# A list scheduler's price table: same-bank PSUM reads put in sequence, a charge for the return to dense products, and other durations re-set

## The chip, the core and the metric

The kernel runs on one core of a Trainium2 chip. Its time is device microseconds (us) from start to end of one execution; three runs of the kernel before are known. One execution was also profiled, and every instruction of it has a start and a duration in the trace. The engines are called as in the profile: PE (TensorE, with PEld for its weight loads), DVE (VectorE), ACT (ScalarE), POOL (GpSimd) and SP (SyncE, which issues the DMAs).

## The reference

One layer of a streaming encoder, for a prompt of 1024 rows and a sample of 32 rows (1056 columns in all, model width 1024), everything in float32:

```
n = rmsnorm(x);  p = n @ w_in                        # 1024 x 3840
x += concat(hgrn2(p[:, :2048]), rwkv7(p[:, 2048:])) @ w_out
x += cross_attention(rmsnorm(x), memory K/V)         # 4 heads of 256, 256 memory rows
x += (silu(n @ w_ff1) * (n @ w_ff3)) @ w_ff2         # n = rmsnorm(x), hidden width 2816
y = rmsnorm(x)
```

`hgrn2` and `rwkv7` are recurrences over time. The kernel computes both by chunks: many small products, element-wise work between them, and a state that goes from chunk to chunk. Memory K and V of the prompt are two more products (`w_ck`, `w_cv`). States, shift rows and memory K/V are outputs too.

## The kernel before

**Products.** A float32 product of full width is made of three float32r products: each operand is split into a high part (an ACT copy) and a low part (a DVE or POOL subtraction), and hi*hi, hi*lo and lo*hi are added up in one PSUM bank (`gemm`, L778; `load_w`, L764; `split`, L798). These are called **dense** here. They have 352 moving columns in the projections, `w_out` and `w_cq`, 264 in `w_co` and the feed-forward part (there with a seven-product scheme, `fast`, L1140), 256 in the memory K/V products. All others are **short** products of the recurrences, the transposes and the attention, in float32 or float16, many on a 64-row or 64-column part of the array.

**Stages.** `run` (L852) records the stages one after the other: the mixers (`mixers`, L1363: the 30 projections of `w_in`, and for each of four head pairs `rwkv`, L1489, and `hgrn`, L1737, each over five pieces of time); memory K/V (`memory_kv`, L886); `out_proj` (L946); `cross` (L962); `ff_hidden` (L1167) and `ff_out` (L1267); `final` (L1338). In the mixers the recurrences are chains of short products with DVE, ACT and POOL work between them, and the dense projections of the next head pairs run beside them on PE. Two places in the chains matter here:

- `inverse` (L1667) inverts small triangular matrices, level by level. At each of four levels DVE reads a PSUM bank to place it on a block diagonal (`place(xbd, ps, self.both)`, L1723; 128x512 in float16) and ACT reads the same bank to copy it (`S.copy(x, ps)`, L1725; 128x256 to float16).
- the state chain of `rwkv` (L1610 to L1628) has three links in each chunk of 64 rows: products `ps_b`, DVE addition; products `ps_sa`, one copy by DVE from partitions 0 to 63 and one by ACT from 64 to 127; products `ps_h`, a DVE multiply-add. The next chunk begins with the result.

**What sets the order.** Nothing is issued while stages are recorded. Each call makes a node of a graph (`record`, L322); `touch` (L161) adds an edge between two nodes that use overlapping parts of one buffer, if one of them writes. A few products in a row are one PE node. Then a list scheduler (`order`, L376) plays the engines forward with clocks of its own: each node costs what `price` (L218) says, an engine switch adds `wait` (L206, table `DELAY`), and a node with a second price, "late", lets its engine go on at once while its result counts as ready later. At each step the engine whose clock is earliest takes, of the nodes that are ready at that clock, the one with the longest remaining path (L557), if buffers and PSUM banks are to be had (`fits`, L490). A stage may start early only when few enough nodes of the earlier stages are left (`LEAD`, L493: 1100 for memory K/V, 250 for `out_proj`). Memory K/V and the projections have a large bias that puts them behind everything else that is ready, so that they fill what is free on PE. The charge for a change of products on PE (`change`, L278) is added to a PE node's cost after the node has been picked (L573).

The result is a fixed order of instructions for each engine, SP included. Every engine runs its own in this order and waits where its next instruction waits, so the planner's prices bear on the chip only through the order. All instructions are emitted by one helper line (L365), so the profile names them by tiles: `bank` is a PSUM bank; `r`, `rw`, `f`, `mb`, `ma`, `wr` are regions of SBUF (`r` holds activations, `rw` split weights, `wr` raw weights, `f`, `mb` and `ma` the rest). A dense projection product is `bank<-r,rw 128x352`; a memory K/V product is `bank<-rw,ma 128x256`.

## Time and profile before

| what | value |
|---|---|
| median of 3 runs | 1962.35 us (1960.7 to 1963.19) |
| time of the profiled execution | 1963.09 us |
| span of its trace (first to last instruction) | 1961.0 us |
| PE busy | 1868.9 us, 95% of the span |
| DVE, ACT, POOL busy | 1402.3, 837.6, 654.7 us |
| mean granted TensorE clock | 0.986 of full speed |

How to read the rows that follow: a row of the windows gives, for a stretch of the span, its length and each engine's busy time in it with the count of instructions, then the granted clock (1.00 is full), the share of time that the DMA engines were busy, and GB/s. A row of the timeline gives the start, the length, the engine, the line, the operation with its tiles and shape, how many equal ones follow each other (x6), and in square brackets how long the engine was idle before and what ended that. A row of the groups ends with the busy time in us, the mean of one instruction in ns, and the idle time before them.

### The profile page before, as it was taken

The numbers are of one execution on the slowest core, as the hardware profiler recorded it, in microseconds if no ns is written. First come the engines' busy times: TensorE is split into PE (matmuls) and PEld (weight loads), VectorE is DVE, ScalarE is ACT, GpSimd is POOL, SyncE is SP. The second block draws the span as 40 slices with busy tenths as digits, with TensorE's granted clock in tenths as the row PEclk, the third lists the DMA queues.
The fourth block names the chain that finished last, engine by engine and source line by source line (L and its number), as shares of the span: only waits on it lengthen the run. The fifth ranks groups of instructions, "written<-read, shape, count | busy, mean of one in ns | idle before, by whom it ended". The sixth has DMA issues, their size and how long they took to land. (4 is left out here: it accounts for less than half of the span.)

```text
span 1961.0 us, 40641 instructions
## 1 busy us (share of the span) xinstructions
PE 1868.9 (95%) x15785; PEld 1731.9 (88%) x15785; DVE 1402.3 (72%) x3112; ACT 837.6 (43%) x2151; POOL 654.7 (33%) x926
## 2 busy tenths in 40 slices
PE   6899999999999999899999999899999999999998
PEld 6788888887788878789899999799999999999997
DVE  4786789659857875634555456797777877968997
ACT  4553545454545455633222235533233333464432
POOL 4632444135424532105400014632332433322421
PEclk9899999999999999899999999899999999999999
DMA  4100110011001101641112122222233224465622
GB/s 144 34 12 26 41 41 23 4 53 29 23 28 45 35 7 52 199 152 34 43 56 64 33 63 88 70 81 93 91 111 117 83 83 137 144 181 168 183 89 89
DMA packets 158111, 149.51 MB, mean 76 GB/s; under 512 B 10080, under 2 KB 146400, under 8 KB 157920
## 3 DMA queue, kind: packets, MB, share of 16 engines
q1 hardware_dynamic: 157920, 146.93, 23.8%
q8 instruction: 124, 2.03, 0.4%
q14 instruction: 67, 0.55, 0.1%
HBM read 111.02 MB, written 35.88 MB: 75 GB/s over the span
## 5 line engine op out<-in xcount | busy, mean ns | idle before, releaser
L365 PE MATMUL bank<-r,rw 128*128 128x264 f32 (+1 forms) x5808 | 928.7, 310 | 29.0 <-DVE rw L365 10.6
L365 PEld LDWEIGHTS bank<-r,rw 128*128 128x128 f32 x5808 | 824.9, 190 | 49.4 <-DVE rw L365 12.3
L365 PE MATMUL bank<-mb,rw 128*128 128x264 f32 (+3 forms) x3456 | 484.4, 293 | 9.0 <-DVE rw L365 7.6
L365 PEld LDWEIGHTS bank<-mb,rw 128*128 128x128 f32 x3456 | 455.9, 189 | 17.4 <-DVE rw L365 11.7
L365 DVE TENSOR_TENSOR f<-bank,f 128x264 f32<-128x264 f32 (+11 forms) x798 | 317.4, 421 | 121.1 <-PE bank L365 114.9
L365 PE MATMUL bank<-f 64*64 64x64 f32 (+8 forms) x2472 | 278.2, 256 | 30.3 <-DVE f L365 14.3
L365 PEld LDWEIGHTS bank<-f 64*64 64x64 f32 (+5 forms) x1675 | 167.2, 155 | 65.4 <-DVE f L365 18.4
L365 POOL TENSOR_TENSOR f<-f 128x2 f32<-128x2 f32 (+8 forms) x167 | 104.6, 637 | 318.9 <-ACT f L365 242.0
L365 ACT ACTIVATE f<-f 128x256 f32<-128x256 f32 (+7 forms) x392 | 158.3, 423 | 112.3 <-DVE f L365 87.5
L365 ACT CAST rw<-wr 128x512 fp32r<-128x512 f32 (+3 forms) x167 | 116.1, 700 | 209.5 <-PE bank L365 132.1
L365 DVE TENSOR_TENSOR f<-f 128x264 f32<-128x264 f32 (+10 forms) x266 | 187.0, 716 | 25.1 <-POOL f L365 12.0
L365 DVE TENSOR_TENSOR rw<-wr,rw 128x512 fp32r<-128x512 f32 (+3 forms) x137 | 109.6, 805 | 43.8 <-ACT rw L365 43.0
L365 ACT CAST rw<-ma 128x512 fp32r<-128x512 f32 (+2 forms) x124 | 70.9, 573 | 153.8 <-POOL ma L365 85.8
L365 ACT COPY f<-bank 128x264 f32<-128x264 f32 (+6 forms) x251 | 87.4, 361 | 111.7 <-PE bank L365 99.6
L365 DVE TENSOR_TENSOR rw<-ma,rw 128x512 fp32r<-128x512 f32 (+2 forms) x124 | 82.5, 672 | 34.2 <-ACT rw L365 34.1
L365 POOL TENSOR_SCALAR f<-f 128x64 f32<-128x64 f32 (+6 forms) x117 | 49.1, 421 | 172.8 <-DVE f L365 104.8
L365 PE MATMUL bank<-f,mb 64*64 64x64 f32 (+9 forms) x982 | 84.9, 241 | 3.8 <-DVE f L365 2.4
L365 ACT CAST f<-bank 128x256 f16<-128x256 f32 (+1 forms) x144 | 46.5, 339 | 87.8 <-PE bank L365 56.9
L365 POOL TENSOR_TENSOR ma<-ma 128x512 f32<-128x512 f32 (+4 forms) x41 | 52.5, 1283 | 90.3 <-DVE rw L365 89.9
L365 ACT ACTIVATE f<-bank,f 128x256 f32<-128x256 f32 (+4 forms) x127 | 52.6, 430 | 69.6 <-DVE f L365 31.2
L365 POOL TENSOR_TENSOR ma<-wr 128x512 f32<-128x512 f32 (+1 forms) x13 | 25.0, 1927 | 161.9 <-DVE rw L365 95.2
L365 DVE TENSOR_TENSOR f<-bank,r 128x264 f32<-128x264 f32 (+1 forms) x56 | 25.2, 464 | 71.8 <-PE bank L365 64.7
(189 smaller groups left out, 2269.2 us busy)
## 6 DMA issues: line engine op xcount, KB each, us to landing
wr<-in_w_in_dram SPq DMA_DIRECT2D x30, 512.0 KB
wr<-in_w_ff_dram SPq DMA_DIRECT2D x27, 512.0 KB
ma<-in_w_ff_dram SPq DMA_DIRECT2D x25, 512.0 KB
h_scratch<-f SPq DMA_DIRECT2D x18, 528.0 KB
f<-h_scratch SPq DMA_DIRECT2D x36, 264.0 KB
ma<-h_scratch SPq DMA_DIRECT2D x34, 264.0 KB
h_scratch<-f SPq DMA_DIRECT2D x12, 396.0 KB
f<-mix_scratch SPq DMA_DIRECT2D x24, 176.0 KB
```

Of the source, the lines that this page charges most:

```text
L365: getattr(eng, method)(*args, **kw)
```

## The change

Only the planner's numbers and edges change; what is computed, the nodes, the buffers and the rule of picking stay.

- `touch` also adds an edge between two reads of overlapping parts of one PSUM bank by different engines, in the order of recording.
- `change` no longer adds 0.03 us wherever either neighbour on PE is not dense; it adds 0.1 us where a dense node follows a short product of certain kinds (`short`).
- An ACT instruction's price goes from 0.18 us (PSUM) or 0.21 us (SBUF) plus 0.83 ns a column to 0.06 or 0.11 us plus the same, with 0.1 us "late".
- POOL's prices change by operation and type, and `DELAY` for ACT and POOL; a DMA is priced at 300 GB/s in place of 200, landing 2.1 us later in place of 1.9.

```diff
-SWITCH, SMALL = 0.095, 0.03
+SWITCH, HIDE = 0.095, 0.1
...
-            if (write or w) and n is not node:
+            if (write or w or self.space == "PS" and n.eng != node.eng) and n is not node:
...
-DELAY = {("vector", "tensor"): 0.2, ("vector", "gpsimd"): 0.18, "vector": 0.115, ("scalar", "tensor"): 0.1,
-         ("scalar", "gpsimd"): 0.05, "scalar": 0.02, ("gpsimd", "tensor"): 0.08, "gpsimd": 0.0, "tensor": 0.21,
+DELAY = {("vector", "tensor"): 0.2, ("vector", "gpsimd"): 0.18, "vector": 0.115, ("scalar", "tensor"): 0.07,
+         ("scalar", "gpsimd"): 0.09, "scalar": 0.04, ("gpsimd", "tensor"): 0.08, "gpsimd": 0.04, "tensor": 0.21,
...
-        return max(0.4, n * out.shape[0] * 4 / 200e3), 1.9
+        return max(0.42, n * out.shape[0] * 4 / 300e3), 2.1
...
-        return (0.18 if args[1].buf.space == "PS" else 0.21) + n * 0.83e-3 + (0.095 if pointer else 0.0), 0.0
+        return (0.06 if args[1].buf.space == "PS" else 0.11) + n * 0.83e-3 + (0.095 if pointer else 0.0), 0.1
     if method == "affine_select":
-        return 0.35, 0.0
+        return 0.36, 0.0
     if method == "memset":
-        return 0.06 + n * 0.5e-3, 0.0
+        return 0.1 + n * 0.8e-3, 0.0
     if method == "tensor_tensor":
-        return 0.13 + n * 2.12e-3 + (0.45 if args[3] == ALU.pow else 0.0), 0.0
+        rounded = out.dtype == F32R and n < 512 or out.dtype == F32 and n in (384, 512)
+        return 0.18 + n * (2.85e-3 if rounded else 2.2e-3) + (0.45 if args[3] == ALU.pow else 0.0), 0.0
     if method == "tensor_scalar":
-        return 0.3 + n * (2.9e-3 if args[4] == ALU.max else 1.3e-3), 0.0
-    return 0.24 + n * 1e-3, 0.0
+        return 0.24 + n * (3.3e-3 if args[4] == ALU.max else 1.1e-3), 0.0
+    return 0.18 + n * 1e-3, 0.0
...
+def short(call):
+    method, args, kw = call
+    if method == "transpose":
+        return args[1].shape[0] <= 64
+    lhs, rhs = kw["lhsT"], kw["rhs"]
+    return lhs.dtype != F32R and (lhs.dtype == F16 or cut_of_array(call) != (False, False) or math.prod(rhs.shape[1:]) < 128)
+
 def change(a, b):
     if a is None:
         return 0.0
-    return (SWITCH if cut_of_array(a.calls[-1]) != cut_of_array(b.calls[0]) else 0.0) + (0.0 if a.dense and b.dense else SMALL)
+    return (SWITCH if cut_of_array(a.calls[-1]) != cut_of_array(b.calls[0]) else 0.0) + (HIDE if b.dense and short(a.calls[-1]) else 0.0)
```

## The prediction

> **What bounds the kernel now.** I read the page first (span and busy time), then the windows, then the waits of PE.
>
> ```profile
> span 1961.0 us, 40641 instructions
> PE 1868.9 (95%) x15785; PEld 1731.9 (88%) x15785; DVE 1402.3 (72%) x3112; ACT 837.6 (43%) x2151; POOL 654.7 (33%) x926
> ```
>
> PE is busy for all but 92.1 us of the span (1961.0 less 1868.9). The change removes no product, so what it can win is idle PE time, and what it can lose is more of it. The windows tell where the 92.1 us lie:
>
> ```profile
> 0.00:100.00 100.00, 77.90 (x481) 71.38 (x482) 58.92 (x129) 51.40 (x122) 54.90 (x127) 0.95 0.30 92
> 100.00:200.00 100.00, 94.77 (x1110) 82.67 (x1110) 75.43 (x184) 47.72 (x139) 31.55 (x69) 0.97 0.05 14
> 200.00:700.00 500.00, 486.51 (x4975) 412.42 (x4974) 381.43 (x1047) 251.65 (x776) 212.49 (x384) 1.00 0.11 32
> 786.00:846.00 60.00, 46.90 (x346) 43.07 (x347) 35.90 (x77) 36.41 (x89) 7.36 (x16) 0.90 0.63 197
> 900.00:1200.00 300.00, 293.77 (x1872) 279.07 (x1871) 157.73 (x377) 93.87 (x226) 55.16 (x54) 0.99 0.17 53
> 1200.00:1300.00 100.00, 87.75 (x649) 84.60 (x648) 81.16 (x143) 50.90 (x125) 50.90 (x44) 0.93 0.21 68
> 1300.00:1700.00 400.00, 396.61 (x3228) 393.45 (x3227) 314.75 (x487) 131.84 (x241) 135.84 (x76) 1.00 0.31 105
> 1700.00:1961.00 261.00, 245.76 (x1930) 239.61 (x1928) 221.74 (x453) 112.06 (x259) 73.33 (x91) 0.99 0.47 145
> ```
>
> The start has 22.1 us of it, the rest of the mixers up to 700 us 18.7 (5.2 and 13.5), their end and memory K/V 13.1, the way into the feed-forward part 12.2, and the last 261 us 15.2. The middle of the mixers, where the planner mixes most, is already 97% busy. That is the frame: no plan can win more than some tens of us.
>
> **The change part by part.** The planner's prices act through the order alone, so I compared the two built orders, engine by engine.
>
> *The charge for a return.* Dense products follow each other every 0.161 us (41 of them from 914.79 to 921.39, 6.60 us):
>
> ```profile
> 914.79 1.45 PE L365 MATMUL bank<-mb,rw 128*128 128x352 f32 x8
> ...
> 921.39 0.65 PE L365 MATMUL bank<-mb,rw 128*128 128x352 f32 x3
> ...
> 251.81 1.23 PE L365 MATMUL bank<-r,rw 128*128 128x352 f32 x6
> 252.88 0.27 PE L365 MATMUL bank<-f 128*32 128x128 f32 x1
> ```
>
> Six of them after short products took 1.07 us to the next start, 0.97 by that spacing: a return costs 0.10, as the new charge says. But the charge is added after a node is picked, so it can't make returns fewer, and it doesn't: the new order has 354 returns, the old 352, and 718 changes between array cuts against 717. Two more at 0.10 are +0.2 us. I take it as nothing.
>
> *Two reads of one bank.* They are in sequence on the chip already. DVE placed from 734.29 to 734.98, ACT began 0.04 us after:
>
> ```profile
> 734.29 0.69 DVE L365 TENSOR_TENSOR mb<-bank,f 128x512 f16<-128x512 f32 x1 [0.33 <-PE bank L365]
> 735.02 0.37 ACT L365 CAST f<-bank 128x256 f16<-128x256 f32 x1 [0.66 <-DVE mb L365]
> ```
>
> The new edges are 116: 36 in the attention, between a maximum and the exponential that needs it anyway, and the 80 of `inverse`. In the old order ACT came first in 25 of the 80; now DVE always does. The ACT copy can come 0.69 us later by that, but its reader waits for two more products and the next placement (another 0.69) in any case: nothing. The two copies of the state chain read different partitions of one bank, so they get no edge, and the planner still has them side by side.
>
> *The durations.* An ACT instruction on 256 columns lasts 0.40 to 0.42 us, but the next one starts after 0.32 and 0.31:
>
> ```profile
> 144.08 0.42 ACT L365 ACTIVATE f<-f 128x256 f32<-128x256 f32 x1 [0.28 <-DVE f L365]
> 144.40 0.40 ACT L365 ACTIVATE ma<-ma 128x256 f32<-128x256 f32 x1
> 144.71 0.40 ACT L365 ACTIVATE f<-f 128x256 f32<-128x256 f32 x1
> ...
> L365 POOL TENSOR_TENSOR r<-f,r 128x352 fp32r<-128x352 f32 x24 | 29.0, 1225 | 92.2 <-DVE f L365 61.4 <-ACT r L365 30.8
> ```
>
> The old price holds ACT for 0.42 us, the new one for 0.32 and 0.1 late: the trace is with the new. A rounded POOL subtraction of 352 columns takes 1.225 us; 0.88 was planned, 1.18 now is. So the plan comes nearer to the chip, and its order differs nearly everywhere in the mixers. From 857 us on it differs little. What this is worth I work out at the places where PE waits.
>
> *Start to the first chains.*
>
> ```profile
> 85.67 0.33 PE L365 MATMUL bank<-f,mb 64*64 64x64 f32 x4 [0.66 <-POOL f L365]
> 89.61 0.70 PE L365 MATMUL bank<-f 128*128 128x256 f32 x2 [3.61 <-DVE f L365]
> 91.13 1.22 PE L365 MATMUL bank<-f 128*128 128x256 f32 x2 [0.82 <-DVE f L365]
> ...
> 141.47 0.40 PE L365 MATMUL bank<-f 64*64 64x64 f32 x4 [1.78 <-DVE f L365]
> 142.41 3.99 PE L365 MATMUL bank<-mb 128*64 128x64 f32 x34 [0.55 <-DVE mb L365]
> ```
>
> The release of the product at 91.13 stands behind 111 DVE instructions in the new order, 115 in the old, with as much PE work before it. Four at about 0.4 us are 1.6; I take **-1.5** (0 to -4.4, the waits of 3.61 and 0.82). In the first state chain the old order has three links with no dense product between them (from 139 to 142.4); the new has a group of six between every two of the first links, 0.97 us each. That covers the 0.55 and half of the 1.78: **-1.5** (0 to -2.3), though what fills here is missing later.
>
> *The middle, 150 to 700 us.* Idle time is 13.5 us in 200 to 700, in many waits under 2 us. The 135 or so links of the state chains that have under 1 us of PE work ahead of them fall from 21 to 17. In that share, 19% of 13.5, it is -2.6; I take **-2** (-8 if truer durations cover most, +4 if the new mix only moves the waits).
>
> *The end of the mixers* is where the new order looks worse.
>
> ```profile
> 781.69 1.12 PE L365 MATMUL bank<-r,rw 128*128 128x352 f32 x6
> 782.64 3.00 PE L365 MATMUL bank<-rw,ma 128*128 128x256 f32 x24
> ...
> 756.72 8.57 SPq L365 DMA_DIRECT2D f<-in_w_ck_dram  x2
> ...
> 797.26 0.47 PE L365 MATMUL bank<-f 128*128 128x128 f32 x1 [3.37 <-ACT f L365]
> ...
> 780.00:790.00 10.00, 8.85 (x67) 8.23 (x66) 9.07 (x25) 7.72 (x21) 3.69 (x8) 1.00 0.62 190
> 790.00:800.00 10.00, 4.83 (x35) 3.85 (x34) 6.46 (x16) 7.24 (x23) 2.46 (x7) 0.85 0.65 194
> 800.00:810.00 10.00, 7.46 (x37) 6.91 (x38) 8.63 (x23) 6.50 (x17) 1.58 (x4) 0.64 0.59 180
> ```
>
> In the old order the last projection is followed at once by memory K/V, whose first two weight tiles had been issued from 756.72 us on, and 51 short products are left to go between. In the new one the projections end earlier, 115 short products follow with nothing dense among them, and the first memory weights are issued only after two tiles of `w_out` and five of `out_proj`'s operands. By the median spacing of such products in the trace these 115 are 18.7 us of PE work. The nearest stretch of before, 780 to 810, is 70% busy (21.14 of 30): 18.7 at 70% is 26.7, a loss of 8.0. Against it, 38 short products fewer than before are left beside memory K/V, and the old 8.9 us of idle there shrinks; I take half, -4.4. Two weight tiles of 512 KB more then go through a stretch that moves 197 GB/s: 1.05 MB, 5.3 us if the transfers bind there; the DMA engines are 63% busy, so I take +1.4. Sum **+5** (-3 if the old idle goes wholly and the DMA doesn't bind, +14 with the 8.0, the 5.3 and some clock).
>
> [...]
>
> ```profile
> 793.00:800.00 7.00, 1.83 (x10) 1.05 (x9) 4.15 (x10) 6.39 (x20) 2.46 (x7) 0.78 0.69 211
> 800.00:804.00 4.00, 2.66 (x10) 2.37 (x11) 3.96 (x11) 3.60 (x12) 0.29 (x1) 0.50 0.57 188
> ```
>
> After seven us in which PE worked for 1.83, the granted clock was 0.50 for the next four. [...]
>
> *Into the feed-forward part.*
>
> ```profile
> 1228.40 5.21 PE L365 MATMUL bank<-r,rw 128*128 128x264 f32 x22 [3.35 <-DVE rw L365]
> ...
> 1251.00:1295.00 44.00, 38.05 (x291) 37.21 (x292) 36.76 (x53) 17.47 (x35) 19.87 (x18) 0.96 0.12 37
> ```
>
> The DVE instruction that releases 1228.40 is number 2081 on DVE in the old order, 2071 in the new: ten fewer ahead, enough to end the 3.35. But the releases near 1251, 1260 and 1295 have the same numbers in both (2118 and 2119, 2127, 2167), and DVE is busy for 36.76 of those 44 us. What isn't done before is owed there: I take **-1** (-3.4 to 0). From there the orders agree but for small moves: 0.
>
> Sum: -1.5 - 1.5 - 2 + 5 - 1 = -1.0 us. On the profiled execution (1963.09, its span and 2.1 around it) that is 1962.1; it ran 0.74 above the median of the three, so on the median 1962.35 it is 1961.3. I predict **1961.0**.
>
> **The rivals.**
> - *The truer plan wins through the mixers.* All its small terms come out at their good ends: -4.4, -2.3, -8, and the end of the mixers costs nothing: -14.7, 1948. For it: ACT and POOL rows, and the thicker chain. Against it: 97% busy there already.
> - *PE runs out of fill* (slower). One place: the 115 short products at the mixers' end. The 8.0 and 5.3 with no return, and 2.7 for ten us at clocks near 0.6: +16; less the 5 us won elsewhere, +11, 1973. It decides if PE is under about 75% busy in that run. For it: 790 to 800 above. Against it: several chains end there together and can cover each other.
> - *The change does nothing that can be measured*: the charge is no part of the pick, 36 of 116 edges are void, and waits only move. That is my forecast's neighbourhood: within 0.2%, about what a measurement of this kernel can tell from no change (1958.4 to 1966.3).
>
> **How the numbers follow.** My forecast, waits that move and cancel (1955 to 1967), gets 0.42: 0.09 of it under 1958.4, 0.31 within, 0.02 above. The truer plan (1943 to 1955) gets 0.27, the lack of fill (1967 to 1980) 0.31. So faster 0.36, same 0.31, slower 0.33. Both signs hold much of the chance; the range takes in most of both, 1945 to 1976.
>
> **What would show it.** Right: PE idle of 15 to 20 us in the 100 us from the last `bank<-r,rw 128x352` of the mixers to `out_proj`, up from 13.1 in 786 to 846; waits gone near 140 and at the first 264-column products; the same idle later. Wrong: a mixers' end as full as before (then the first rival), or memory K/V products that wait for DMA (then the second). If idle time changes after 1300 us, I have missed where the orders differ.

## The result, and the profile after

The changed kernel takes 1968.97 us (median of 8 runs, 1966.92 to 1974.39) against 1962.19 us for the kernel before, measured beside it (8 runs): ratio 1.0036, 95% interval 1.0024 to 1.0049. It is slower, by 6.8 us or 0.36%: a small loss, but 1 lies outside the interval. I had put 0.42 on waits that move and cancel, 1961.0 us; the time lies in the range of 1945 to 1976.

The page of the changed kernel, span and busy time:

```profile
span 1967.9 us, 40633 instructions
...
PE 1874.4 (95%) x15785; PEld 1735.9 (88%) x15785; DVE 1406.3 (71%) x3112; ACT 826.1 (42%) x2150; POOL 666.0 (34%) x926
```

PE was idle for 92.1 us before (1961.0 less 1868.9) and is now for 93.5 (1967.9 less 1874.4). So of 6.9 us of span only 1.4 are idle time, and 5.5 are a PE that is *busy* for longer with the same 15785 products. That already says where to look: at the granted clock. Its mean over the profiled execution is 0.986 before and 0.977 after; as the clock records of both traces hold only 1.00 and 0.50, that is about 55 and 91 us at half clock. The windows, in the columns of the prediction (length, busy PE, PEld, DVE, ACT, POOL, granted clock, DMA share, GB/s):

```profile
0.00:100.00 100.00, 82.25 (x550) 74.94 (x550) 63.52 (x140) 51.08 (x125) 59.08 (x133) 0.95 0.30 92
100.00:200.00 100.00, 96.14 (x1138) 82.43 (x1137) 81.45 (x211) 52.41 (x167) 36.76 (x76) 1.00 0.07 19
200.00:700.00 500.00, 480.12 (x4838) 407.10 (x4838) 367.29 (x1005) 239.59 (x751) 204.19 (x367) 0.98 0.10 31
786.00:846.00 60.00, 49.26 (x329) 45.03 (x330) 37.26 (x92) 36.79 (x101) 11.09 (x25) 0.77 0.70 218
900.00:1200.00 300.00, 292.31 (x1844) 277.89 (x1843) 157.63 (x372) 93.72 (x227) 59.19 (x56) 0.99 0.17 53
1200.00:1300.00 100.00, 88.38 (x659) 85.18 (x658) 79.37 (x139) 54.21 (x132) 50.96 (x46) 0.93 0.21 65
1300.00:1700.00 400.00, 396.83 (x3228) 394.72 (x3227) 315.36 (x490) 129.13 (x234) 140.84 (x76) 1.00 0.31 105
1700.00:1967.00 267.00, 251.99 (x1988) 245.37 (x1986) 228.55 (x464) 115.65 (x267) 78.41 (x93) 0.99 0.46 144
```

Against the rows of before: up to 200 us PE is idle for 21.6 us in place of 27.3; from 200 to 700 for 19.9 in place of 13.5; from 786 to 846 for only 10.7 in place of 13.1, but at a clock of 0.77 in place of 0.90. From 900 us on nothing differs by over 1.5 us.

Windows at fixed times compare different work. So here and below I also use the **extra time** at a point of PE's work: the products are counted in their order, each at the median distance between starts that its kind has in the trace of before (a dense 352-column one 0.161 us), and the extra time is the start of the product there less that sum. Waits, slow clocks and slow releases are all in it.

| stretch of PE's work, us | extra before | extra after | difference | the prediction's terms there |
|---|---|---|---|---|
| 0 to 150 | 45.2 | 33.7 | -11.5 | -1.5 and -1.5 |
| 150 to 650 | 31.3 | 44.1 | +12.8 | -2 |
| 650 to 750 | 19.8 | 27.6 | +7.8 | +5 |
| 750 to the end | 51.9 | 51.0 | -0.9 | -1 |

With 1.7 us less work by that count (1803.1 against 1801.4) this is +6.5, of the 6.9 by which the spans differ. The change wins more at the start than I thought possible, gives all of it back in the middle, and loses at the mixers' end. How the loss divides between the second and the third row depends on how finely the kinds of product are told apart; by coarser kinds more of it falls to the second.

**The start.** Both kernels, 0 to 160 us (before first):

```profile
0.00:160.00 160.00, 132.87 (x1127) 119.67 (x1128) 109.57 (x245) 81.41 (x204) 79.12 (x172) 0.95 0.21 65
```

```profile
0.00:160.00 160.00, 139.47 (x1300) 124.66 (x1301) 117.01 (x263) 85.61 (x222) 84.72 (x177) 0.97 0.21 65
```

In the same 160 us PE starts 1300 products in place of 1127, and DVE is busy for 7.4 us more.

**The middle.** Before, from 160 to 350 and from 600 to 660 us, and the same of the changed kernel:

```profile
160.00:350.00 190.00, 187.23 (x2008) 158.61 (x2008) 148.38 (x403) 98.65 (x306) 79.46 (x151) 1.00 0.10 28
...
600.00:660.00 60.00, 58.31 (x554) 49.88 (x553) 46.12 (x127) 25.83 (x83) 33.78 (x55) 1.00 0.18 53
```

```profile
160.00:350.00 190.00, 180.65 (x1865) 152.78 (x1864) 141.96 (x395) 92.60 (x296) 74.83 (x147) 0.98 0.10 28
...
600.00:660.00 60.00, 55.03 (x431) 48.41 (x431) 48.15 (x120) 25.28 (x80) 33.59 (x58) 0.91 0.16 47
```

Both stretches lose busy time and clock. The worst place in the first, in the timeline of PE and the windows of the changed kernel:

```profile
316.61 0.29 PE L375 MATMUL bank<-f,ma 128*128 128x64 f16 x4
...
320.14 0.33 PE L375 MATMUL bank<-f 64*64 64x64 f32 x4 [1.44 <-DVE f L375]
...
322.25 0.58 PE L375 MATMUL bank<-ma 128*128 128x64 f16 x8 [1.56 <-DVE ma L375]
...
328.89 1.23 PE L375 MATMUL bank<-r,rw 128*128 128x352 f32 x6
...
320.00:325.00 5.00, 3.30 (x37) 2.85 (x38) 4.97 (x13) 3.05 (x7) 2.63 (x7) 0.57 0.00 0
325.00:330.00 5.00, 4.66 (x54) 3.42 (x52) 4.47 (x13) 1.74 (x4) 4.81 (x4) 0.75 0.31 90
```

From 316.6 to 328.9 PE starts no dense product, DVE is busy for 9.44 of the 10 us from 320 to 330, and the clock is at half from 320.7 to 327.5. The worst place in the second:

```profile
641.38 3.13 DVE L375 SCALAR_TENSOR_TENSOR f<-f 128x256 f32<-128x256 f32 x1
...
641.82 2.33 POOL L375 TENSOR_TENSOR rw<-wr,rw 128x1024 fp32r<-128x1024 f32 x1
...
645.17 3.81 PE L375 MATMUL bank<-f 128*128 128x64 f16 x39 [2.62 <-DVE f L375]
648.91 2.13 PE L375 MATMUL bank<-r,rw 128*128 128x352 f32 x6
```

A DVE instruction on 256 columns lasts 3.13 us (the 66 of its kind and shape in the kernel before take 0.54 us in the mean), and ends 0.36 us after a POOL subtraction on 1024 columns that began beside it. PE has no dense product from 640.7 to 648.9, waits 2.62 us for DVE, and is at half clock from 644.9 to 651.8.

**The end of the mixers.** The timeline of PE (last projection, short products, first memory K/V product) and of SP:

```profile
773.47 1.21 PE L375 MATMUL bank<-r,rw 128*128 128x352 f32 x6
...
794.14 2.16 PE L375 MATMUL bank<-f 128*128 128x128 f32 x7 [5.86 <-DVE f L375]
797.52 0.79 PE L375 MATMUL bank<-f 128*128 128x128 f32 x2 [1.23 <-DVE f L375]
...
800.84 9.19 PE L375 MATMUL bank<-f 128*128 128x128 f32 x42
809.68 0.56 PE L375 MATMUL bank<-rw,ma 128*128 128x256 f32 x1
```

```profile
790.23 5.81 SPq L375 DMA_DIRECT2D f<-mix_scratch  x5
...
802.54 0.38 SPq L375 DMA_DIRECT2D f<-in_w_ck_dram  x1
```

```profile
788.00:800.00 12.00, 4.88 (x20) 3.42 (x20) 7.98 (x29) 6.31 (x23) 4.29 (x13) 0.51 0.61 180
800.00:805.00 5.00, 5.00 (x26) 4.52 (x27) 2.94 (x9) 3.52 (x13) 0.41 (x2) 0.50 0.24 77
805.00:810.00 5.00, 5.00 (x25) 4.59 (x24) 2.60 (x8) 2.72 (x9) 0.94 (x2) 0.50 0.63 188
810.00:816.00 6.00, 4.57 (x23) 4.33 (x22) 4.64 (x13) 3.73 (x17) 3.10 (x4) 0.53 0.72 226
816.00:826.00 10.00, 9.98 (x78) 8.89 (x77) 6.15 (x12) 7.18 (x16) 0.95 (x2) 1.00 0.83 258
```

The last projection ends at 774.7 us, and the first load of memory K/V's weights is issued only at 802.54, 27.8 us later (before: at 756.72, 26 us *ahead* of the last projection's end at 782.8). In between PE has short products alone, stands still for 5.86 us up to 794.14, and is at half clock from 788.3 on, for 27.3 us. From 800 to 810 it is busy all the time, and still at 0.50.

### The profile page after: what moved, and what is told of

It is laid out like the page before. It is cut to its first block, busy times and chain, and to the rows that moved or that the text cites. A ratio compares the mean times of both kernels' runs of the same rounds, so it can differ in the third digit from the quotient of the medians.

```text
span 1967.9 us, 40633 instructions
## 1 busy us (share of the span) xinstructions
PE 1874.4 (95%) x15785; PEld 1735.9 (88%) x15785; DVE 1406.3 (71%) x3112; ACT 826.1 (42%) x2150; POOL 666.0 (34%) x926
## 4 chain that ended last, share of the span: by engine, by line
PE 72%; DVE 16%; issue 4%; POOL 4%; ACT 3%; DMA 1%; DVEq 0%; ACTq 0%; SPq 0%; POOLq 0%
PE bank L375 72%; DVE f L375 9%; POOL f L375 2%; DVE rw L375 2%; DVE ma L375 2%; DVE mb L375 2%; ACT f L375 2%; POOL mb L375 1%; DMA f<-h_scratch 1%; ACT mb L375 1%; POOL rw L375 0%; DVE r L375 0%; ACT rw L375 0%; POOL ma L375 0%; ACT ma L375 0%
## 5 line engine op out<-in xcount | busy, mean ns | idle before, releaser
L375 PE MATMUL bank<-r,rw 128*128 128x264 f32 (+1 forms) x5856 | 945.6, 311 | 27.9 <-DVE rw L375 9.4
L375 PE MATMUL bank<-mb,rw 128*128 128x264 f32 (+4 forms) x3408 | 478.6, 293 | 7.2 <-DVE rw L375 6.5
L375 DVE TENSOR_TENSOR f<-bank,f 128x264 f32<-128x264 f32 (+10 forms) x766 | 310.2, 426 | 153.2 <-PE bank L375 146.0
L375 PE MATMUL bank<-f 128*128 128x64 f16 (+7 forms) x2574 | 287.1, 258 | 34.9 <-DVE f L375 21.7
L375 PEld LDWEIGHTS bank<-f 128*128 128x128 f32 (+3 forms) x1718 | 173.6, 160 | 69.6 <-DVE f L375 23.4
L375 POOL TENSOR_TENSOR f<-f 128x2 f32<-128x2 f32 (+7 forms) x160 | 101.8, 647 | 298.1 <-ACT f L375 241.6
L375 DVE TENSOR_TENSOR f<-f 128x264 f32<-128x264 f32 (+9 forms) x224 | 136.7, 623 | 14.5 <-POOL f L375 6.0
L375 PEld LDWEIGHTS bank<-f,mb 128*128 128x128 f32 (+6 forms) x874 | 62.5, 147 | 22.0 <-DVE f L375 7.3
L375 ACT CAST rw<-f 128x512 fp32r<-128x512 f32 (+3 forms) x71 | 45.9, 650 | 80.1 <-PE bank L375 70.1
L375 DVE TENSOR_TENSOR ma<-bank,f 128x512 f16<-128x512 f32 (+9 forms) x139 | 61.8, 458 | 24.6 <-PE bank L375 23.8
L375 ACT ACTIVATE f<-bank,f 128x256 f32<-128x256 f32 (+4 forms) x127 | 52.4, 431 | 59.3 <-DVE f L375 33.4
```

The costliest lines, as they stand in the source:

```text
L375: getattr(eng, method)(*args, **kw)
```

## The experiments

The theories, which the expectations spell out further: *gap*, that the loss is the stretch at the mixers' end in which PE has only short products; *prices*, that one part of the change costs by itself; *draw*, that each set of prices draws another order, whose losses have little to do with the prices' truth. Two more came up on the way: *page*, that what counts at the mixers' end is when the first weights of memory K/V are loaded, and *rows*, that the loads and splits of memory K/V's rows disturb the middle. The table gathers all runs; extra time is as above, from one profiled run each, and the last column is the issue of the first memory K/V load against the end of the last projection, in us.

| kernel | median, us | ratio to before, 95% | extra 0-150 | 150-650 | 650-750 | first load |
|---|---|---|---|---|---|---|
| before | 1962.2 | | 45.2 | 31.3 | 19.8 | -26.1 |
| after | 1969.0 | 1.0024 to 1.0049 | 33.7 | 44.1 | 27.6 | +27.8 |
| e1 charge alone | 1994.6 | 1.0145 to 1.0176 | 45.7 | 40.6 | 47.0 | +41.5 |
| e2 before, 1 ns | 1993.4 | 1.0147 to 1.0182 | 52.4 | 41.3 | 38.4 | +33.0 |
| e3 without charge | 1951.4 | 0.9924 to 0.9951 | 35.1 | 37.6 | 16.1 | -18.5 |
| e4 fill | 1976.5 | 1.0054 to 1.0081 | 36.9 | 44.3 | 22.8 | +16.5 |
| e9 charge 0.11 | 1956.3 | 0.9959 to 0.9983 | 34.4 | 29.0 | 27.2 | -5.1 |
| e10 charge 0.095 | 1971.9 | 1.0034 to 1.0080 | 37.0 | 30.3 | 37.9 | +62.7 |
| e6 GpSimd alone | 1970.8 | 1.0027 to 1.0058 | 43.2 | 34.1 | 22.8 | -13.0 |
| e5 read order alone | 1985.3 | 1.0094 to 1.0130 | 44.9 | 48.1 | 33.6 | +1.9 |
| e11 after, free page | 1960.2 | 0.9976 to 0.9999 | 36.9 | 47.5 | 17.3 | -65.8 |
| e12 before, free page | 1963.5 | 0.9997 to 1.0016 | 43.0 | 32.1 | 20.5 | -79.2 |
| e13 before, late load | 1976.8 | 1.0053 to 1.0083 | 44.5 | 30.5 | 35.7 | +15.9 |
| e14 read order, free page | 1976.6 | 1.0051 to 1.0085 | 46.8 | 44.7 | 29.7 | -74.9 |
| e15 charge 0.11, free page | 1951.8 | 0.9928 to 0.9953 | 31.9 | 37.7 | 18.7 | -70.2 |
| e16 ScalarE and DMA | 2008.3 | 1.0206 to 1.0263 | 46.0 | 51.3 | 40.4 | +42.2 |
| e7 DMA alone | 1989.6 | 1.0121 to 1.0148 | 42.1 | 40.6 | 34.9 | +27.7 |
| e17 after, rows late | 1958.2 | 0.9966 to 0.9987 | 36.4 | 44.9 | 11.9 | -75.2 |
| e18 without GpSimd | 1958.3 | 0.9970 to 0.9991 | 32.8 | 28.2 | 18.7 | -8.1 |
| e19 without read order | 1978.1 | 1.0068 to 1.0099 | 42.0 | 50.0 | 25.9 | +2.4 |

How far can one profiled run be trusted? Three runs with the order of before up to 686 us of work (before, e12, e13) have 31.3, 32.1 and 30.5 in the second column; four with that of the changed kernel up to 571 (after, e4, e11, e17) 44.1, 44.3, 47.5 and 44.9. But e9 and e15 share an order up to 678 and have 29.0 and 37.7. A difference under 9 us in that column is not told from chance here; the 12.8 between before and after is, as three runs of the one order and four of the other lie apart.

### The charge by itself, one nanosecond, and the change without the charge

e1 is the kernel before with the new `change` and `short`, nothing else. e3 is the changed kernel with the old `change` (SMALL = 0.03). e2 is the kernel before with the price of a float16 product raised by 1 ns:

```diff
-            return max(0.029, n / 2400 + 0.002), 0.0
+            return max(0.029, n / 2400 + 0.003), 0.0
```

> Only the charge for a return to dense products is changed, the other prices and edges are as before. Its built order has the same feature as the changed kernel: after the last projection 19.1 us of short products stand on PE with no dense product among them (18.7 in the changed kernel, none before). Theory 'gap' (this run of short products, through idle PE and the half clock that follows it, is what makes the change slower): half-speed clock for 15 us or more in that stretch, and 1964 to 1972 us. Theory 'prices' (a price nearer to the trace makes a better plan; the slower end comes from another part of the change): at or under 1962 us. Theory 'every plan is a new draw' (any shift of the planner's clocks gives another order, several us up or down through the whole mixers): a time anywhere from 1954 to 1974, not tied to the gap.

> The kernel before with one planned duration raised by 1 ns (a float16 product, 0.003 in place of 0.002 us of fixed cost): no price is nearer to the trace by that in any way that counts. Its order has a gap of 17.6 us of short products after the last projection. 'Gap': 1964 to 1971 us with a half-speed spell of 15 us or more at the end of the mixers. 'Prices': as before, 1960 to 1964 us. 'Every plan is a new draw': anywhere from 1954 to 1974.

> The whole change without the new charge (the old charge stays). Its order has a gap of 0.8 us, and the first memory K/V weights are issued early, as before. 'Gap': the early gain of the changed kernel (12.7 us at its best, near 157 us) may or may not last, but the end of the mixers costs no more than before (17.9 us of PE time over its work from the last projection to the first product of out_proj), and the kernel is at or under 1963 us. 'Prices': between the changed kernel and before, 1963 to 1968 us. 'Every plan is a new draw': anywhere from 1954 to 1974.

Measured: 1994.6, 1993.4 and 1951.4 us. The charge alone costs 32 us, and taking it out of the change wins 17.6 us and beats the kernel before by 10.8. But 1 ns in a price of the kernel before, which makes it neither truer nor falser in a way that counts, costs 31 us, nearly as much as the charge, and the most of it in the same place: in e1 and e2 the first load goes out 41.5 and 33.0 us behind the last projection, and 650 to 750 us of work cost 47.0 and 38.4 in place of 19.8. So a charge need not be wrong to cost this. The times of e1 and e2 lie some 20 us above what any theory had put down, and e3 fits *gap*'s at or under 1963 and lies under the 1954 of *draw*: the draws reach further than I thought.

### Dense products put into the gap

e4 is the changed kernel with 72 products more that nothing reads (12 groups of six, 264 columns), which the planner may put between the last projection and memory K/V. So it does more work than the reference needs.

```diff
+        for _ in range(12):
+            nc.cut()
+            ps = self.psg.tile([128, 512], F32, tag="g", name="ps_fill")[:, :264]
+            for k in range(6):
+                nc.tensor.matmul(ps, lhsT=self.xh[:, k, 0:128], rhs=self.xh[:, k + 1, 0:264], start=k == 0, stop=k == 6-1)
...
```

> The changed kernel with 72 more dense products of 264 columns (12 groups of six, 0.73 us each by the trace's spacing of 0.122, 8.8 us in all) whose result nobody reads, placed by the planner into the gap of short products, one group about every 2 us; the order ahead of the gap is the same. 'Gap by the half clock': with dense products in it the half-speed spell of 27.3 us shrinks to 10 us or less, the first memory K/V product starts no later than in the changed kernel (809.7 us) in spite of 8.8 us of more work, and the time is 1964 to 1970 us. 'Gap by waiting alone' (the chains of the recurrences end when they end, whatever the clock): the memory K/V products start within 2 us of 809.7 and the time stays at 1967 to 1971 us. 'Work is work': 8.8 us later, 1976 us or more.

Measured: 1976.5 us, 7.5 more than the changed kernel. The filler is about 8.4 us of work by the count (1809.8 against 1801.4). The time at half clock between the last projection and `out_proj` falls from 27.3 to 17.1 us and the extra time from 650 to 750 by 4.8, but the filler itself is paid for, as the theory *work is work* had it. How much of the 4.8 is the clock, this run doesn't tell: the first load goes out sooner in it too (16.5 us behind the last projection in place of 27.8).

### Other charges, and two other parts alone

e9 and e10 change one digit; e6 is the kernel before with POOL's new prices and POOL's own delay of 0.04; e5 is the kernel before with the new edges in `touch` alone.

```diff
-SWITCH, HIDE = 0.095, 0.1
+SWITCH, HIDE = 0.095, 0.11      # e10: 0.095
```

> The change with a charge of 0.11 us in place of 0.1. Nothing else differs, and the plan that comes of it has 1.7 us of short products between the last projection and the first memory key product, where the changed kernel has 18.7. Theory 'gap' (the loss is that TensorE has only short products left there, idles and falls to half clock): the half-clock spell of 27 us near 790 goes, the wait that builds up between 700 and 750 us of TensorE work falls from 23.2 to 15 to 19, and the time is 1951 to 1962. Theory 'the charge itself costs, whatever the size' (a higher price for a return to dense products pushes short work together): 1969 or more. Theory 'each plan is a new draw': the tail as by 'gap', but the two places at 315 to 349 us and 617 to 650 us, where the changed kernel gave back 5 to 6 us each, lie elsewhere or are gone, so the time may differ by some 10 us more either way. In all of them the first chains keep their gain: wait at 150 us of work near 34, against 45 in the kernel before.

> The change with a charge of 0.095 us in place of 0.1: 39.8 us of short products between the last projection and the first memory key product, the most of any plan here. Theory 'gap': a longer spell at half clock than the changed kernel's 27 us, a wait between 700 and 750 us of work of 35 or more, and 1980 to 2000. Theory 'the charge itself costs': it is 5 per cent smaller, so the time stays near 1969 or falls a little. The first chains keep their gain (wait near 34 at 150 us of work) by either.

> The kernel before with GpSimd's new durations alone (its delay with them): 0.8 us of short products in the place of the gap, and no gap. If the gain of the first chains comes of ScalarE's durations, it isn't here: wait at 150 us of work near 45, and with a tail like that of the kernel before the time is 1957 to 1966. If any of the new durations brings it, the wait there is near 35 and the time near 1951.

> The kernel before with the order of two engines' reads of one PSUM bank alone, no new price. 0.8 us of short products in the place of the gap. By the prediction's reason (the readers stand in that order in nearly all places anyway) and with the gain of the first chains tied to ScalarE's durations: wait at 150 us of work near 45, no long half-clock spell, 1957 to 1966. If the order itself costs or gains, the wait at 150 or in the two middle places (315 to 349 and 617 to 650) differs from the kernel before by over 3 us.

Measured: 1956.3, 1971.9, 1970.8 and 1985.3 us. A charge of 0.11 makes the kernel faster than before, 0.1 and 0.095 slower: the time doesn't go by the charge's size. And the middle of both other orders, 29.0 and 30.3, has none of the 12.8 us that the changed kernel loses there, with the same prices but for that digit. (e15, which shares e9's order there, has 37.7, so part of e9's 29.0 is chance; the two together still lie under all four runs of the changed kernel's order.) That speaks for *draw* and against *prices*. e6 and e5 had been put at 1957 to 1966; both missed, e5 by 19 us.

*Gap* as I had put it fails three times. e9 has next to no short products standing alone (1.7 us), yet 27.2 us of extra time at the end; e5 has 0.8 us of them and 33.6; and e10, with 39.8, comes out at 1971.9, under the 1980 it was to have, though its end costs the 35 or more that *gap* had put down (37.9). The loads of e9 tell why:

```profile
758.62 0.38 SPq L375 DMA_DIRECT2D f<-in_w_ck_dram  x1
789.97 0.38 SPq L375 DMA_DIRECT2D f<-in_w_ck_dram  x1
```

One load goes out early, the second 31 us later. In e5 the first comes 1.9 us behind the last projection, at 795.50. It isn't how many short products stand alone that counts, but when the weights of memory K/V come. So far that is a reading of three runs; the next four test it. From here on the theory is *page*.

### The page that isn't free

A tile of memory K/V's raw weights takes 16 units of SBUF, beside a reserve of 32 that must stay free, and the planner places it in one whole free page of 16. Its own account, read from `fits` and `place`: in the kernel before the load is refused, nearly always for lack of units, until 714.1 us of the planner's clock, when a page is free; in the changed one at about 718 there are 48 free units but no whole page, later up to 78, and the load is refused until 737.9. e11 lets these loads lie in the two pages of the projections' weights too, which are free by then:

```diff
-HOME = {"keep": ("f0", "r0"), "wr": ("wr",),
+HOME = {"keep": ("f0", "r0"), "wm": ("f0", "ma", "mb", "wr"), "wr": ("wr",),
```

A class with an entry in `HOME` is also freed of the reserve. The planner's account tells the two apart for the changed kernel: freed of the reserve alone the load stays at 738.1, and with the two pages but the reserve kept it goes out at 674.2. It is the pages that let it go; on the chip only the two together were run. e12 is the kernel before with the same entry, e14 is e5 with it. e13 goes the other way: the kernel before with a larger reserve for memory K/V, so that its first load comes later.

```diff
-RESERVE = [64, 32, 24, 24, 24, 24, 24]
+RESERVE = [64, 40, 24, 24, 24, 24, 24]
```

> The changed kernel, but the loads of memory K/V's weights may also lie in the two pages that the projections' weights use (one more entry in HOME). The order is that of the changed kernel, instruction for instruction on every engine, up to 675 us of TensorE work; behind it the first of these loads is issued at 629 us of work in place of 708, and 2.9 us of short products stand alone in place of 18.7. Theory 'page' (the plan leaves no whole page free for the first load, 48 to 66 small units but not one page, so memory K/V starts late, TensorE has only short products and falls to half clock): the wait from 650 to 750 us of work falls from 27.6 to 16 to 20, the 27 us spell at half clock goes, the time is 1956 to 1962. Theory 'the last chains bound it' (VectorE and the chains through it set when the mixers end, whatever TensorE has beside them): 1966 or more. In both the wait at 650 us stays near 78, as in the changed kernel.

> The kernel before with the same entry. Its order stays the same up to 708 us of TensorE work but for these loads, which go out from 629 us in place of 684; no short products stood alone there before. Theory 'page': little to win, the wait from 650 to 750 falls from 19.8 to 14 to 19, time 1956 to 1962. Theory 'every new order moves the time by 10 to 20 us': outside of 1952 to 1970.

> The kernel before, with memory K/V's reserve raised from 32 to 40 units and nothing else: the order is the same up to 686 us of TensorE work, the first of its loads moves from 684 to 709 us of work, and 10.1 us of short products then stand alone ahead of memory K/V. None of the changed prices is in it. Theory 'page': the wait from 650 to 750 rises from 19.8 to 28 to 38, time 1970 to 1980. Theory 'the changed prices cost': 1962, as before.

> The order of two reads of one bank alone (1985.3 us), with the loads of memory K/V's weights allowed in the projections' pages. The order is the same up to 679 us of TensorE work; the first load goes out at 632 us of work in place of 700. Theory 'page': the wait from 650 to 750 falls from 33.6 to 16 to 20, time 1968 to 1973; what is left above the kernel before is the 14 us that it lost between 600 and 650 us. Theory 'the order of the reads itself costs at the end of the mixers': 1980 or more.

Measured: 1960.2, 1963.5, 1976.8 and 1976.6 us. From 780 to 820 us, in this order: before, after, e11 and e13.

```profile
780.00:820.00 40.00, 31.15 (x217) 27.67 (x215) 28.37 (x76) 26.07 (x76) 9.33 (x22) 0.87 0.59 183
```

```profile
780.00:820.00 40.00, 30.54 (x204) 25.77 (x204) 26.47 (x82) 27.52 (x93) 12.82 (x26) 0.66 0.49 146
```

```profile
780.00:820.00 40.00, 35.38 (x300) 30.39 (x296) 27.16 (x79) 27.42 (x89) 16.95 (x28) 0.91 0.47 145
```

```profile
780.00:820.00 40.00, 24.45 (x139) 20.00 (x138) 27.88 (x82) 27.25 (x83) 9.98 (x25) 0.70 0.54 166
```

DVE does nearly the same in all four (26.5 to 28.4 us): it isn't DVE that decides. PE starts 300 products in e11 and 139 in e13. e11 takes 8.8 us from the changed kernel, its end falls from 27.6 to 17.3 as *page* had it, and the 27 us at half clock are gone (from 770 to 870 us its windows have about 6.8, at 0.92 and 0.74 from 790 to 810; its profiled run, 1966.45 us, lies 6.3 above its median; it has 6.6 us more extra time before 650 than that of the changed kernel, in the same order). e13 has none of the new prices and loses 14.7 us, and its columns differ from those of before in the end alone (35.7 in place of 19.8): the loss goes with the late load and needs none of the prices. Its first load on SP, and PE ahead of it:

```profile
796.68 0.38 SPq L365 DMA_DIRECT2D f<-in_w_ck_dram  x1
```

```profile
788.86 2.12 PE L365 MATMUL bank<-f 128*128 128x128 f32 x9 [7.67 <-DVE f L365]
```

e12 shows that the free page wins nothing where the load was early anyway (not even the little that was expected: 20.5 at the end, and 1963.5 us). e14 is a half miss: 8.7 us are won, but its end keeps 29.7, not 16 to 20. What keeps it dear is open. PE waits there for copies of the last loads (issued from 853.6 us on):

```profile
855.80 0.58 PE L365 MATMUL bank<-rw,ma 128*128 128x256 f32 x1 [2.59 <-ACT rw L365]
...
863.72 0.38 PE L365 MATMUL bank<-rw,ma 128*128 128x256 f32 x1 [1.50 <-ACT rw L365]
```

These two, 4.1 us, are all the waits of its memory K/V products for ACT; the kernel before has 5.2 us of them, so they don't explain it.

### Do the gains add; where the start's gain comes from; the rows of memory K/V

e15 joins e9 and the free page. e16 is the kernel before with ACT's new prices and delays and the DMA's prices; e7 has the DMA's alone. e17 is e11 with memory K/V kept out until 500 of the mixers' steps are left:

```diff
-LEAD = {0: BIG, 1: 1100, 2: 250, 3: 400, 4: 100, 5: 200, 6: 200}
+LEAD = {0: BIG, 1: 500, 2: 250, 3: 400, 4: 100, 5: 200, 6: 200}
```

> The change with a charge of 0.11 (1956.3 us by itself) and the loads of memory K/V's weights allowed in the projections' pages. The order is that of the 0.11 kernel up to 678 us of TensorE work; its first load goes out at 629 us of work in place of 695. Theory 'page': the wait from 650 to 750 us of work falls from 27.2 to 16 to 20, time 1946 to 1951. Theory 'gains don't add' (what the load no longer delays, the last chains do): 1954 or more.

> The kernel before with ScalarE's new durations and the DMA's, no other part of the change. Theory 'ScalarE's durations bring the early gain': wait at 150 us of TensorE work 33 to 38, against 45 in the kernel before. Theory 'GpSimd's or the read order bring it together with them': 43 or more. The end of the mixers has 28.5 us of short products by themselves and its first load at 694, so by 'page' the wait from 650 to 750 is 25 to 38; with a middle like that of one plan or the other, the time is 1955 to 1980.

> The kernel before with the DMA's new durations alone. Theory 'ScalarE's durations bring the early gain': wait at 150 us of work 43 to 47, as in the kernel before; if the DMA's bring it, 33 to 38. By 'page' the end of the mixers is dear here too (first load at 710 us of work, 11.4 us of short products alone): wait from 650 to 750 of 33 to 45, time 1973 to 1990.

> The changed kernel with the pages as in the free-page run, and memory K/V not let in before 500 of the mixers' steps are left (1100 in the others): its order is that of the changed kernel up to 571 us of TensorE work, where that one puts in memory K/V's rows (571 and 585 us); here they come at 703. Theory 'rows' (their work on VectorE, ScalarE and GpSimd among the last heads makes the wait of 9 us between 550 and 600 us of work): that wait falls to 3 to 5, and the time is 1952 to 1957, 1960 less what falls. Theory 'the mixers' own order there': the wait stays 7 to 9 and the time 1958 to 1963.

Measured: 1951.8, 2008.3, 1989.6 and 1958.2 us. The free page takes 4.6 us from e9 and its end falls from 27.2 to 18.7, within what *page* said, though the time is just above the 1946 to 1951 expected of it.

e16 refutes what I held of the start: ScalarE's prices and the DMA's without the order of reads don't bring the gain (46.0). It also lies 28 us above the 1980 it was to stay under, the dearest order of all. e7 came out as *page* and the first theory had it: 42.1 at the start, 34.9 at the end, a first load 27.7 us behind the last projection.

e17 refutes *rows*: from 600 to 660 us it does as badly as the changed kernel's 55.03 us at 0.91, while e9 (second fence) has a full PE there:

```profile
600.00:660.00 60.00, 54.88 (x422) 48.23 (x420) 47.39 (x119) 26.63 (x84) 33.50 (x60) 0.91 0.14 41
```

```profile
600.00:660.00 60.00, 59.68 (x670) 49.09 (x666) 48.49 (x123) 32.70 (x103) 26.72 (x51) 1.00 0.14 41
```

### Which parts the start needs

e18 is the changed kernel with POOL's old prices and its old delay of 0.0; e19 is the changed kernel without the new edges in `touch`.

> The change without GpSimd's new durations and delay. Theory 'ScalarE's and GpSimd's together': the first 150 us of work lose the gain, wait 43 or more there. Theory 'ScalarE's and the order of reads together': 33 to 38. By 'page' (first load at 694 us of work, 1.4 us of short products alone) the wait from 650 to 750 is 22 to 28. Time 1953 to 1966 with the gain, 1963 to 1978 without.

> The change without the order of two engines' reads of one bank. Its order is that of the changed kernel up to 77 us of TensorE work. Theory 'ScalarE's and GpSimd's together': wait at 150 us of work 33 to 38. Theory 'ScalarE's and the order of reads together': 43 or more. By 'page' (first load at 703 us of work, 0.8 us of short products alone) the wait from 650 to 750 is 27 to 35. Time 1955 to 1968 with the gain, 1965 to 1980 without.

Measured: 1958.3 and 1978.1 us. The extra time at 150 us is 32.8 in e18 and 42.0 in e19. From 0 to 160 us, e18 first:

```profile
0.00:160.00 160.00, 141.06 (x1271) 125.98 (x1272) 114.45 (x261) 84.02 (x218) 84.72 (x178) 0.95 0.21 65
```

```profile
0.00:160.00 160.00, 136.34 (x1147) 122.06 (x1148) 112.32 (x253) 80.95 (x208) 82.52 (x175) 0.95 0.21 65
```

GpSimd's prices aren't needed for the gain; the order of reads is, and beside it the prices of ScalarE, of the DMA, or both. All orders with these (after, e3, e4, e9, e10, e11, e15, e17, e18) have 31.9 to 37.0; all that lack the order of reads or the prices (before, e1, e2, e5, e6, e7, e12, e13, e14, e16, e19) 42.0 to 52.4. No run has the order of reads with ScalarE's numbers alone, for which the planner finds no order that fits, or with the DMA's alone, so which of the two it takes is open. By what steps they shorten the first chains, no run isolates. By *page* the ends of e18 and e19 were to cost 22 to 28 and 27 to 35; with 18.7 and 25.9 both are a little cheaper.

## Why the prediction was wrong, point by point

- **The charge for a return: 0.** Right in what it said, that the charge can't make returns fewer. Wrong in its consequence: the charge moves the planner's clock and so redraws all that follows. With 0.03 by the old rule the change takes 1951.4 us, with 0.095, 0.1 and 0.11 it takes 1971.9, 1969.0 and 1956.3.
- **Two reads of one bank: 0.** Wrong by itself and together. Alone it costs 23 us (e5); in the change it is needed for the gain of the start (42.0 without it in e19, 33.7 with it). I had costed the 116 edges where they stand and not the order that they lead to.
- **Start to the first chains: -1.5 and -1.5.** Right in sign; measured -11.5 up to 150 us of work. I had priced two waits, with -6.7 as their best end; the whole stretch from 0 to 160 us went faster, with 173 more products started in it. That the sign was right is in part luck: I had put nothing on the order of reads, which the gain needs.
- **The middle: -2 (-8 to +4).** This is the step that failed. Measured +12.8, outside its bounds: with -2 here and the other rows as measured, the span would have come out 7.9 us shorter in place of 6.9 longer. The step took the share of chain links with little PE work ahead as a measure of the idle time, and that got better (21 to 17). What the order lost shows in two stretches, 315 to 349 and 617 to 650 us: in each PE has no dense product at hand for 8 to 12 us while DVE is busy nearly all the time (11.71 of 12.3 us and 8.01 of 8.2), and 6.8 us at half clock come with it. The share of links counted neither how long such a stretch is nor the clock. Neither the prices nor the charge as such make these: e10, one digit away, doesn't lose there (30.3), and e9 and e15, with another digit, lose less (29.0 and 37.7). Why this order has them is open; the rows of memory K/V are excluded (e17), and the slow DVE instruction beside POOL's at 641 us was seen, not tested.
- **The end of the mixers: +5 (-3 to +14).** Measured +7.8 from 650 to 750 us of work: right in place, sign and about in size. The mechanism was half seen. I had the short products standing alone and the late loads both, and put the price on the first; e5, e9, e11 and e13 show that it goes by the loads, and the planner's account that in the changed kernel these wait for a whole page. Two numbers of the sum were loose: the 1.4 for the transfers is not worked out from anything, and 8.0 less the old idle of 8.9 is -0.9, not the bound of -3. The sign that I named for it was wrong: I looked for 15 to 20 us of idle PE from the last projection to `out_proj`. It is idle there for 11.8 us (89.9 less 78.11), before 13.3 (75.5 less 62.16). The loss is in a busy PE at a low clock, in a stretch 14.4 us longer (before first):

```profile
782.80:858.30 75.50, 62.16 (x468) 58.09 (x467) 43.20 (x92) 44.24 (x102) 9.88 (x23) 0.91 0.63 198
...
774.70:864.60 89.90, 78.11 (x606) 71.14 (x607) 51.58 (x123) 53.57 (x140) 14.68 (x31) 0.85 0.61 191
```

- **The clock: no term of the sum**, only of the bound of +14 and of the second rival (ten us near 0.6). It was 27.3 us at 0.50. The one place of before that I had shown, PE busy for 1.83 of seven us and half clock behind, doesn't foretell such a spell: it was of 10.2 us (797.0 to 807.2), 7.2 of them the 0.64 from 800 to 810. In the changed kernel the records have the fall at 788.3, at the start of the wait of 5.86 us, with PE busy for 2.09 of the 3 us from 785 to 788. Work alone didn't end it soon: PE was busy from 800 to 810 us and the clock stayed at 0.50 until 815.6. What the spell cost can't be told from the load: e11, which has neither the long spell nor the late load, has 10.3 us less at the end.
- **Into the feed-forward part: -1.** Measured -0.9 from 750 us of work to the end. After 1300 us nothing moved, as said.
- **The rivals.** The second (PE runs out of fill) had the place, half of the mechanism and the direction, with 1973 us; its own condition, PE under about 75% busy in that run, just failed (26.97 of the 35.0 us from 774.7 to 809.7, 77%, but at a clock of 0.69). The first had the start's win (-6.7 of its -14.7; measured -11.5). Both happened, and the middle took the difference. The failure of the judgement was to let terms of opposite sign cancel to -1.0 in the likeliest case: the 20 kernels of the table spread from 1951 to 2008 us.

**A version that beats both**: e3 (the change without the charge), 1951.4 us, 0.9924 to 0.9951 of the kernel before; e15 is as fast (1951.8). e18 is 16.6 us ahead at 750 us of work (79.7 against 96.3) and gives back 13 of it behind, mostly from 1400 us on; where from wasn't pursued.

## What to carry to other kernels

A price in a list scheduler acts through the whole order behind it: 1 ns cost 31 us here, so one run of a changed price says little about whether the price is true, and several neighbouring values (0.095, 0.1, 0.11) belong to every such test. Before pricing an order, look for the resource that lets the next stage's first transfer go: here room for one weight tile. An earlier first load won 4.6 to 8.8 us in e15, e14 and e11, a later one cost 14.7 in e13, each with the prices as they were. And read busy time together with the granted clock: a stretch can have *less* idle time and take longer (the mixers' end: 11.8 us of it in place of 13.3, in 89.9 us in place of 75.5, at a clock of 0.85 in place of 0.91).

## What the runs showed of the hardware that I had not expected

A TensorE that was busy mostly with short products stayed at half clock far longer than the wait at which it fell. In the changed kernel it was 27.3 us, 10 of them (800 to 810) without any idle time, at a wait of 5.86; in e16 PE was busy for 26.74 of 31 us at 0.50:

```profile
785.00:816.00 31.00, 26.74 (x188) 21.65 (x188) 16.41 (x53) 8.95 (x36) 5.38 (x14) 0.50 0.13 39
...
805.00:812.00 7.00, 7.00 (x40) 5.61 (x39) 1.46 (x6) 1.75 (x8) 0.92 (x2) 0.50 0.00 0
812.00:816.00 4.00, 4.00 (x24) 3.33 (x22) 1.23 (x5) 1.44 (x8) 1.47 (x4) 0.51 0.57 162
```

There the clock came back at 815.9 us, after 11 us with no idle at all and before the first dense product (821.3). In e13 it came back at 795.7, 6.8 us into short products that began at 788.86. So in e13 and e16 the clock returned without a dense product, and in the changed kernel and e16 it was still at 0.50 after ten us of a busy PE; what decides is open. The wait at the fall was not long everywhere either: in the changed kernel it came at 320.7 us, where PE waited for 0.90, 1.44 and 1.56 us, and in e16 at 785.2, where no wait was over 1.56 us.

The spells have a grain. The clock records of the two traces, before and after, hold 24 spells at half clock ahead of the last one of each: 15 of 3.41 us, seven of 6.83, one of 10.24 and one of 27.31, all whole multiples of 3.413 us. The spell of e16, 785.2 to 815.9, is 30.7 us, nine of them. What makes the grain, no run shows.
